# Output projection of a hybrid decoder layer: two tiles at once, seven block products in place of eight

## The chip, the cores and the metric

The kernel runs on one core of one Trainium2 chip. Each core has a matrix engine (PE, whose weight loads are shown as PEld), VectorE (DVE), ScalarE (ACT), GpSimd (POOL), and a queue engine (SP) that issues most transfers. Each engine works through its own instructions in order and waits on semaphores for the others. Results of PE land in PSUM (eight banks of 128x512 f32); everything else lies in SBUF or, outside the core, in DRAM. The metric is the device time of one execution in microseconds (us).

## The reference, cut to what matters

One decoder layer over 2048 tokens of width 1024, in f32. The change sits in the last two lines: `y` is 2048 x 1024, `w_out` is 1024 x 1024.

```python
h = rms_norm(x, pre_norm_g)
proj = h @ w_in                       # columns: a_u, a_v, sq, sk, sv, mq, z
y_a = chunked_spatial_gating(gelu(a_u), gelu(a_v), ...)   # 4 groups of 128 channels
y_b = sliding_window_attention(sq, sk, sv, sinks, rel_bias)
y_c = memory_cross_attention(mq, mk, mv)                  # 256 memory tokens
y = concatenate([y_a, y_b, y_c]) * silu(z)
x = x + rms_norm(y @ w_out, post_norm_g)
```

## The kernel before

The tokens are taken in four tiles (`t` = 0..3) of `TS` = 512. PE multiplies in a format that keeps only part of an f32 value, so each operand is split (`split`, L74 to L76) into a high part, rounded by ScalarE, and a low part, the difference, made by VectorE or GpSimd; a product is then three matmuls, high x high, high x low and low x high. One matmul here is 128x128 weights by 512 columns.

Weights come in units of 128 x 1024. `order` (L79 to L87) lists all units of all tiles in the order of use, and `weight_unit` (L129) keeps four units ahead: at first a unit is loaded as f32 from the input (`load_unit`, into the three places tagged `wraw`), split into one of four places tagged `whl`, and the split pair (1 MB) is stored to `split_d` in DRAM; later tiles load the pair from there. SP issues all of these, in program order.

A tile runs in stages:

- `v`: four units, 96 matmuls into four PSUM banks of the pool `ps_mm`, then GELU and normalisation on ACT, DVE and POOL.
- the groups `sv`, `k`, `q`, `mq`, `z`, `u` (`group`, L225), each 24 matmuls. Between the parts of a group, `slot()` runs pieces of the attention units: every unit of the window or memory attention has three stages (logits and softmax; transpose and split; product with the values), placed at fixed slot numbers by `A_SLOTS`. A tile has 60 slots, tile 0 has 68. What the slots issue for PE and SP stands in program order; the order on ACT, DVE and POOL is set by a planner that simulates the program.
- `finish` (L596) and `gate_a` (L647) make the eight 128-channel pieces of `y`, each split at once into the tile `y`.
- the output projection of the tile (L682 to L724): two halves `hf` of 512 output columns, 96 matmuls each into four banks `op`; while it runs, `load_h` (L217) loads, scales and splits the next tile's normalised `x` into `hT`, of which there is only one. Each half is squared (L715, for the norm) and multiplied by the norm's gain (L723) into `osb`; at the end `osb` is scaled, added to a fresh load of `x` and stored (L742 and, in the last tile, L749 to L755).

PE and SP follow the program's order exactly (`manual_schedule`).

Of the kernel before, what the change touches and what calls it, by code (L numbers as in the profile page):

```python
# [33 lines left out]
O_ORDER = (0, 2, 3, 1)  # L34
# [5 lines left out]
def kernel(  # L40
# [19 lines left out]
    cp = ctx.enter_context(tc.tile_pool(name="cp", bufs=1))  # L60
    wp = ctx.enter_context(tc.tile_pool(name="wp", bufs=4))
    sp = ctx.enter_context(tc.tile_pool(name="sp", bufs=2))

    tiny = ctx.enter_context(tc.tile_pool(name="tiny", bufs=2))
# [15 lines left out]
    for t in range(NT):  # L80
# [6 lines left out]
        order += [(U_O + 4 * hf + j, t) for hf in range(2) for j in O_ORDER]  # L87
# [5 lines left out]
    split_d = dram.tile([U_MK, P, 2, D], F32, name="split_d")  # L93
    stored_at = {u: 1 if u < U_SV else NT if u < U_MQ else 0 for u in range(U_MK)}
# [5 lines left out]
    def load_unit(i):  # L100
        u, t = order[i]
        if t > stored_at.get(u, 0):
            return
        raws[i] = raw_tile(f"wraw_{t}_{u}")
        for c in (slice(0, 512), slice(512, D)) if i == 0 else (slice(0, D),):
            nc.sync.dma_start(raws[i][:, c], wst[u][:, c])
            yield

    def split_unit(i):
        u, t = order[i]  # L110
        if i >= len(order) - 4:

            j = 2 * (i - len(order) + 4)
            w = hT[:, :, j : j + 2, :].rearrange("p s k n -> p s (k n)")
        else:
            w = wp.tile([P, 2, D], F32R, tag="whl", name=f"whl_{t}_{u}")
        ready[u, t] = w
        if i not in raws:
            nc.sync.dma_start(f32(w), split_d[u])
            return  # L120
# [8 lines left out]
    def weight_unit(u, t):  # L129

        i = order.index((u, t))
        while halved[0] < min(i + (4 if i < len(order) - 8 else 5), len(order)):
# [23 lines left out]

    ident = cp.tile([P, P], F32, name="ident")
# [20 lines left out]
    hT = cp.tile([P, 2, KC, TS], F32R, name="hT")  # L178
# [18 lines left out]
    def along(rstd, t):  # L197
# [5 lines left out]
        bcs = sp.tile([P, TS], F32, tag="bcs", name=f"bcs_{t}", bufs=1)  # L203
# [3 lines left out]
    def split_h(xk, k, bcs):  # L207

        g = g_pre[:, k : k + 1]
# [7 lines left out]
    def load_h(t, k, bcs):  # L217
        xk = sp.tile([P, TS], F32, tag="xk", name=f"xk_{t}_{k}", bufs=2)
        nc.sync.dma_start(xk, xT[t, k])
        split_h(xk, k, bcs)  # L220
# [4 lines left out]
    def group(w, t, tag, pool=None, slot=None):  # L225
# [4 lines left out]
        n = 0  # L230
        for k in range(KC):
# [13 lines left out]
    gpost_bc = cp.tile([P, D], F32, name="gpost_bc")  # L245
# [9 lines left out]
    def load_constants():  # L255
# [3 lines left out]
        nc.sync.dma_start(gpost_bc, gpost.broadcast_to([P, D]))  # L259
# [40 lines left out]
    def prep_memory():  # L300
# [14 lines left out]
        mT = sp.tile([P, 2, KC, MEM], F32R, tag="y", name="mT", bufs=1)  # L315
# [179 lines left out]

    for t in range(NT):

# [12 lines left out]
        for j in range(4):  # L510
            if t == 0:
                for kk in range(2):
                    split_h(xj[j][:, kk, :], 2 * j + kk, None)
# [7 lines left out]
            steps = [(i, *s) for i in range(4) for s in passes] if j == 3 else [(i, *s) for s in passes for i in range(4)]  # L521
            for i, hi, wi, kk in steps:
# [3 lines left out]
                                 stop=(j == 3 and (hi, wi, kk) == passes[-1]))  # L526
            if t == 0 and j == 0:
# [68 lines left out]
        def finish(name, k, z):  # L596

            for i in range(2):
                o = O[name][:, i, :]

                nc.vector.scalar_tensor_tensor(o, o, 0.5, ZB[z + i], ALU.mult, ALU.mult)
                split(y[:, 0, k + i, :], y[:, 1, k + i, :], o)
# [16 lines left out]
        at = [0]  # L619

        def slot(_=None):
            for stage, n in sorted(stages.pop(at[0], [])):
# [24 lines left out]
        def gate_a(g):  # L647
# [13 lines left out]
            split(y[:, 0, g, :], y[:, 1, g, :], af)  # L661
# [7 lines left out]
        y = sp.tile([P, 2, KC, TS], F32R, tag="y", name=f"y_{t}", bufs=1)  # L669
# [4 lines left out]
        if t + 1 < NT:  # L674
            for rstd_next in token_stats(t + 1):
                pass
        gate_a(2)
        gate_a(3)
        assert not stages


        rls = []  # L682
        ssp = tiny.tile([P, 2, 4], F32, tag="ssp", name=f"ssp_{t}")
        osb = [sp.tile([P, D], F32, tag=f"S{i}", name=f"osb_{t}_{i}", bufs=1) for i in range(4)]
        for hf in range(2):
            pool, tag = (ps_t, "t") if hf else (ps_mm, "mm")
# [147 lines left out]
```

## Time and profile before

| | |
|---|---|
| median of 3 runs | 799.35 us (798.95 to 799.65) |
| profiled execution, its own time | 799.43 us |
| its span, first to last instruction | 797.7 us |
| mean granted clock of PE | 0.993 |
| busy: PE / DVE / ACT / POOL | 783.7 / 496.2 / 368.4 / 160.9 us |
| moved by DMA | 169.05 MB, mean 212 GB/s |

The stages on PE, from the trace (us from the span's start): tile 0 up to its output projection 0 to 178.2, then the projection to 222.7; tile 1 to 368.9 and its projection to 413.3; tile 2 to 558.4 and to 602.9; tile 3 to 747.8 and to 791.5. The views are read like this: a row of the windows gives for a stretch its length, then each engine's busy time with its number of instructions, PE's granted clock, the DMA engines' busy share and rate. A row of the timeline gives start, duration, engine, line, operation, output<-inputs, shape and count, and in brackets the idle time before it with what ended it. A row of a tile gives the smallest, median and largest duration in ns. Busy time of PE counts overlapped, pipelined instructions, so a busy PE need not be at its peak rate.

### The profile page before, as it was taken

How to read it: one execution, taken by the hardware profiler on the slowest of the kernel's cores; microseconds unless marked ns; L12 is line 12 of the kernel's file. 1: busy time of each engine (PE TensorE's matmuls, PEld its weight loads, DVE VectorE, ACT ScalarE, POOL GpSimd, SP SyncE). 2: the span in 40 equal slices, each digit the busy share in tenths (PEclk: the TensorE clock that was granted, in tenths of full speed). 3: DMA queues.
4: the chain of work that ended last, by engine and by line, in shares of the span. 5: the costliest groups of instructions: out<-in, count | busy, mean ns of one | idle time of the engine just before them, and what ended most of it. 6: DMA issues, size and time to landing. Idle time of an engine off the chain costs nothing.

```text
span 797.7 us, 10520 instructions
## 1 busy us (share of the span) xinstructions
PE 783.7 (98%) x3884; PEld 660.0 (83%) x3884; DVE 496.2 (62%) x920; ACT 368.4 (46%) x816; POOL 160.9 (20%) x139
## 2 busy tenths in 40 slices
PE   9999999999999999999999999999999999999996
PEld 7878877888887888888888888888888888888885
DVE  6497899886546567775524466775624646777322
ACT  7785755753425544562314633473211653444221
POOL 4565442322223122000002203100000402200002
PEclk9999999999999999999999999999999999999999
DMA  8866465594898543555776453463759354334642
GB/s 324 312 219 221 141 239 185 202 370 144 321 358 322 208 159 128 207 194 184 246 295 226 161 184 129 159 229 141 257 217 375 121 191 159 123 142 159 234 188 105
DMA packets 36275, 169.05 MB, mean 212 GB/s; under 512 B 4187, under 2 KB 4736, under 8 KB 23936
## 3 DMA queue, kind: packets, MB, share of 16 engines
q1 hardware_dynamic: 33680, 160.97, 55.7%
q10 hardware_dynamic: 2544, 7.41, 2.3%
q8 instruction: 30, 0.49, 0.2%
q14 instruction: 21, 0.17, 0.1%
HBM read 132.71 MB, written 35.66 MB: 211 GB/s over the span
## 4 chain that ended last, share of the span: by engine, by line
PE 61%; issue 11%; DVE 7%; DMA 5%; POOL 2%; ACT 2%; SPq 0%; DVEq 0%; POOLq 0%; ACTq 0%
PE g_z L233 16%; PE op L694 12%; PE g_u L233 8%; PE v L523 5%; PE g_q L233 4%; PE g_mq L233 4%; DMA split_d<-whl 4%; PE g_k L233 2%; PE o_c L471 1%; PE l_b L400 1%; PE g_sv L233 1%; PE o_b L434 1%; PE l_c L450 1%; PE tp_c L465 1%; PE sg L652 1%
## 5 line engine op out<-in xcount | busy, mean ns | idle before, releaser
L233 PE MATMUL g_z<-hT,whl 128*128 128x512 f32 x768 | 196.0, 399 | 0.0
L233 PEld LDWEIGHTS g_z<-hT,whl 128*128 128x128 f32 x768 | 140.2, 191 | 25.7
L694 PE MATMUL op<-whl,y 128*128 128x512 f32 x672 | 153.9, 390 | 0.0
L694 PEld LDWEIGHTS op<-whl,y 128*128 128x128 f32 x672 | 125.7, 188 | 25.8
L76 POOL TENSOR_TENSOR whl<-wraw,whl 128x1024 fp32r<-128x1024 f32 x36 | 87.4, 2432 | 163.9 <-ACT whl L75 145.8
L233 PE MATMUL g_u<-hT,whl 128*128 128x512 f32 x384 | 97.2, 395 | 0.0
L523 PE MATMUL v<-whl,hT 128*128 128x512 f32 x384 | 88.6, 390 | 0.3 <-DVE hT L212 0.3
L523 PEld LDWEIGHTS v<-whl,hT 128*128 128x128 f32 x384 | 72.0, 188 | 16.4 <-DVE hT L212 0.7
L75 ACT CAST whl<-wraw 128x1024 fp32r<-128x1024 f32 (+1 forms) x51 | 52.7, 1033 | 66.3 <-DMA wraw<-in_wst 32.1
L233 PEld LDWEIGHTS g_u<-hT,whl 128*128 128x128 f32 x384 | 69.4, 188 | 12.9
L723 DVE TENSOR_TENSOR osb<-op,gpost_bc 128x512 f32<-128x512 f32 x32 | 21.4, 687 | 54.5 <-ACT jk L715 54.5
L715 ACT ACTIVATE jk<-op 128x512 f32<-128x512 f32 x32 | 19.0, 598 | 68.1 <-PE op L694 68.1
L424 POOL TENSOR_SCALAR_AFFINE_SELECT pp_b<-po_b 128x512 fp32r<-128x512 f32 x30 | 19.9, 664 | 141.5 <-ACT po_b L75 141.5
L233 PE MATMUL g_q<-hT,whl 128*128 128x512 f32 x192 | 45.9, 394 | 0.0
L233 PE MATMUL g_mq<-hT,whl 128*128 128x512 f32 x192 | 44.7, 389 | 0.0
L410 ACT ACTIVATE Lc_b<-Lc_b,nm_b 128x129 f32<-128x129 f32 x64 | 25.0, 393 | 42.4 <-DVE nm_b L408 42.4
L233 PEld LDWEIGHTS g_q<-hT,whl 128*128 128x128 f32 x192 | 35.7, 188 | 7.8 <-issue 0.5
L233 PEld LDWEIGHTS g_mq<-hT,whl 128*128 128x128 f32 x192 | 35.9, 188 | 7.3
L457 ACT ACTIVATE L_c<-l_c,nm_c 128x256 f32<-128x256 f32 x64 | 29.8, 471 | 26.1 <-DVE nm_c L455 26.0
L214 DVE SCALAR_TENSOR_TENSOR xk<-xk,colt,bcs 128x512 f32<-128x512 f32 x24 | 21.9, 949 | 17.2 <-DMA xk<-in_xT 16.8
L75 ACT CAST hT<-xk 128x512 fp32r<-128x512 f32 x24 | 14.9, 621 | 37.1 <-DVE xk L214 36.7
L153 POOL TENSOR_TENSOR rsr_o<-rsa_o,mhalf 128x4 f32<-128x4 f32 x3 | 3.0, 1013 | 139.0 <-DVE rsa_o L151 139.0
(181 smaller groups left out, 1229.4 us busy)
## 6 DMA issues: line engine op xcount, KB each, us to landing
whl<-split_d SPq DMA_DIRECT2D x70, 1024.0 KB, 4.8
split_d<-whl SPq DMA_DIRECT2D x26, 1024.0 KB, 8.1
wraw<-in_wst SPq DMA_DIRECT2D x49, 512.0 KB, 5.5
xs<-in_x SPq DMA_DIRECT2D x12, 512.0 KB, 4.1
xk<-in_xT SPq DMA_DIRECT2D x24, 256.0 KB, 3.1
xv<-in_x SPq DMA_DIRECT2D x8, 512.0 KB, 6.7
xr<-in_x SPq DMA_DIRECT2D x8, 512.0 KB, 8.1
hT<-split_d SPq DMA_DIRECT2D x4, 1024.0 KB, 8.9
```

The lines of the kernel that those rows point to most:

```text
L75: nc.scalar.copy(hi, src)
L76: (lo_engine or nc.vector).tensor_tensor(lo, src, f32(hi), ALU.subtract)
L214: nc.vector.scalar_tensor_tensor(xk, xk, g, bcs, ALU.mult, ALU.mult)
L233: nc.tensor.matmul(ps, w[:, wi, k * P : (k + 1) * P], hT[:, hi, k, :], start=(n == 0), stop=(n == 3 * KC - 1))
L400: nc.tensor.matmul(lg[:, e, :], S[kv][:, e, c * P : (c + 1) * P], KK[:, kv, s, c * P : c * P + 256], start=(s == 0), stop=(s == 1))
L410: nc.scalar.activation(Lc[:, h, : P + 1], Lc[:, h, : P + 1], AF.Exp, bias=nm[:, h : h + 1], accum_out=den[:, h : h + 1])
L424: nc.gpsimd.affine_select(prev[:, s], f32(own[:, s]), [[0, 4], [-1, P]], ALU.is_gt, 0.0, base=0, channel_multiplier=1)
L457: nc.scalar.activation(p[:, e, :], lg[:, e, :], AF.Exp, bias=nm[:, e : e + 1], accum_out=den[:, e : e + 1])
L523: nc.tensor.matmul(vps[i], hT[:, hi, 2 * j + kk, i * P : (i + 1) * P], w[:, wi, kk * 512 : (kk + 1) * 512], start=(j == 0 and (hi, wi, kk) ...
L694: nc.tensor.matmul(ops[i], y[:, hi, k, i * P : (i + 1) * P], w[:, wi, kk * 512 : (kk + 1) * 512], start=(j == O_ORDER[0] and kk == 0 and h ...
L715: nc.scalar.activation(junk, ops[i], AF.Square, accum_out=ssp[:, hf, i : i + 1])
L723: nc.vector.tensor_tensor(half, ops[i], gpost_bc[:, hf * 512 : (hf + 1) * 512], ALU.mult)
```

## The change

The output projection leaves the tile loop. In the loop each piece of `y` is stored to DRAM as f32 (`store_y`, six ticks later by `flush_y`; a tick is a slot) and not split. There are two places for `h` (`hTs`), so that `load_h` of the next tile runs in slots of the present one: in its last 28 slots the statistics, then `along`, then one `load_h` every second slot. Behind the last tile the pools of the loop are closed and a second phase does the projection for two tiles at a time (`p` = 0: tiles 0 and 1; `p` = 1: tiles 2 and 3). With A the 1024 x 1024 block of `y` of the two tiles and B the weights, both cut into 2 x 2 blocks of 512 x 512, it forms seven products for the eight of the plain form (each sum on VectorE, in two halves of 128 x 1024):

```
S1 = A21 + A22   S2 = S1 - A11   S3 = A11 - A21   S4 = A12 - S2
T1 = B12 - B11   T2 = B22 - T1   T3 = B22 - B12   T4 = B21 - T2
products, in order: S2.T2, S3.T3, A11.B11, A12.B21, S1.T1, A22.T4, S4.B22
```

Each product is 4 row blocks (`m`) of 12 matmuls; X and Y are banks that two products accumulate into. The weight operands (B11, B21, B22, T1 to T4, each in two halves) are made, split and stored to DRAM in slots of tiles 1 and 2 (`weight_operands`); S2 and S3 of the first pair in slots of tile 3 (`first_sums`). The eight units of the output weights no longer stand in `order`; T2 and T3 are its last four units. The core of the diff:

```diff
-        order += [(U_O + 4 * hf + j, t) for hf in range(2) for j in O_ORDER]
+    order += [("T2", 0), ("T2", 1), ("T3", 0), ("T3", 1)]
+    hTs = [hp.tile([P, 2, KC, TS], F32R, name=f"hT{i}") for i in range(2)]
+    def weight_operands(j, place):
...
+        def operand(op, r):
+            w = place[:, :, 2 * (n[0] % 4) : 2 * (n[0] % 4) + 2, :].rearrange("p s k n -> p s (k n)")
+            n[0] += 1
+            split(w[:, 0], w[:, 1], r, nc.gpsimd)
+            to_store.append((op, w))
...
+        def minus(out, a, b):
+            nc.vector.tensor_tensor(out, a, b, ALU.subtract)
...
+            by_bank = j == 3 or (j == 0 and t > 0)
...
-                nc.vector.scalar_tensor_tensor(o, o, 0.5, ZB[z + i], ALU.mult, ALU.mult)
-                split(y[:, 0, k + i, :], y[:, 1, k + i, :], o)
+                nc.vector.scalar_tensor_tensor(ZB[z + i], O[name][:, i, :], 0.5, ZB[z + i], ALU.mult, ALU.mult)
+                store_y(t, k + i, ZB[z + i])
...
+            for i in range(4):
+                jobs.setdefault(n_slots - 28 + 2 * i, []).append(stats_next)
+            jobs.setdefault(n_slots - 18, []).append(along_next)
+            for k in range(KC):
+                jobs.setdefault(n_slots - 17 + 2 * k, []).append(lambda k=k: load_h(t + 1, k, late["bcs_next"]))
+        if t:
+            side = first_sums(hTs[0]) if t == NT - 1 else weight_operands(t - 1, hTs[1 - t % 2]) if t < 3 else iter(())
+            for s in range(4, 32):
+                jobs.setdefault(s, []).append(lambda: next(side, None))
...
-            split(y[:, 0, g, :], y[:, 1, g, :], af)
+            store_y(t, g, af)
...
+    def operand(name, p):
+        A = {n: yraw[n, p] for n in ("11", "12", "21", "22") if (n, p) in yraw}
+        w = p2.tile([P, 2, 4, TS], F32R, tag="yop", name=f"yop_{name}_{p}", bufs=2)
+        for k in range(0, 4, 2):
...
+            split(w[:, 0, ks], w[:, 1, ks], src)
+    def norm_half(o, c, ss, col, p, tag):
+        nc.scalar.activation(junk, o[:, c], AF.Square, accum_out=ss[:, col : col + 1])
+        nc.vector.tensor_tensor(o[:, c], o[:, c], gpost_bc[:, c], ALU.mult)
+    def finish_rows(o, ss, xr, t, m, ends):
+        nc.vector.tensor_scalar(a, ss[:, 0:1], 1.0 / D, EPS, ALU.mult, ALU.add)
+        nc.vector.scalar_tensor_tensor(a, ss[:, 1:2], 1.0 / D, a, ALU.mult, ALU.add)
+        nc.gpsimd.tensor_tensor(r, a, mhalf2[:, 0:1], ALU.pow)
+        for c in (lo, hi) if ends else (slice(0, D),):
+            nc.vector.scalar_tensor_tensor(o[:, c], o[:, c], r, xr[:, c], ALU.mult, ALU.add)
+            (nc.sync if ends and c is lo else nc.scalar).dma_start(out[r0 : r0 + P, c], o[:, c])
...
+        for m in product(X, s2, pieces(T2), True):
+            nc.scalar.copy(osa[m][:, hi], X[m])
+        for m in product(X, s3, pieces(T3), False):
+            nc.scalar.copy(osb[m][:, lo], X[m])
...
+        for m in product(Y, a11, rows(B11), True):
+            nc.vector.tensor_tensor(osa[m][:, hi], Y[m], osa[m][:, hi], ALU.add)
+            nc.vector.tensor_tensor(osb[m][:, lo], osb[m][:, lo], Y[m], ALU.add)
...
+        for m in product(X4, a22, rows(T4), True):
+            nc.vector.tensor_tensor(osb[m][:, lo], X4[m], osb[m][:, lo], ALU.add)
+            norm_half(osb[m], lo, ssb[m], 0, p, f"b{m}_{p}_0")
+            finish_rows(osb[m], ssb[m], xrs[m], tb, m, False)
+            xrs.append(residual_load(*((tb, 3) if m == 0 else (ta, m - 1))))
+            if m == 1:
+                s4 = operand("S4", p)
+                if p == 0:
+                    load_y("22", 1)
+                    load_y("11", 1)
+        for m in product(Z, s4, rows(B22), False):
+            nc.vector.tensor_tensor(osa[m][:, hi], Z[m], osa[m][:, hi], ALU.add)
+            norm_half(osa[m], hi, ssa[m], 1, p, f"a{m}_{p}_1")
+            finish_rows(osa[m], ssa[m], xrs[4 + m], ta, m, p == 1 and m == 3)
+            if p == 0 and m == 1:
+                s2_next = operand("S2", 1)
+                load_y("12", 1)
+        if p == 0:
+            s3_next = operand("S3", 1)
+            B11 = load_operand("B11", 1, 0)
```

309 lines of the change are left out of this document (210 added, 99 removed).

## The prediction, written before the changed kernel ran

> **What bounds the kernel now.** I read the totals first, then the windows cut at the stages.
>
> ```profile
> span 797.7 us, 10520 instructions
> PE 783.7 (98%) x3884; PEld 660.0 (83%) x3884; DVE 496.2 (62%) x920; ACT 368.4 (46%) x816; POOL 160.9 (20%) x139
> 0.00:178.19 178.19, 170.96 (x873) 143.72 (x874) 146.12 (x242) 118.02 (x235) 77.28 (x53) 0.98 0.68 245
> 222.66:368.86 146.20, 145.59 (x742) 123.33 (x741) 93.44 (x191) 70.11 (x169) 26.29 (x27) 1.00 0.58 212
> 368.86:413.33 44.47, 44.47 (x201) 36.94 (x201) 19.82 (x30) 11.43 (x26) 0.00 (x0) 1.00 0.69 249
> 413.33:558.43 145.10, 145.10 (x741) 123.22 (x741) 89.11 (x189) 67.38 (x161) 21.55 (x25) 1.00 0.51 185
> ```
>
> PE bounds it: it sits idle 14.0 us in all, 7.2 of them in tile 0. VectorE is at 82% in tile 0, at 64% and 61% in the loops of tiles 1 and 2, and at 45% in a projection. So a projection (44.5 us) is also the time in which VectorE catches up, and this is what the change takes out of the loop. Next the rate of PE, from the chain that ended last:
>
> ```profile
> 375.21 38.12 PE op L694 x168
> ```
>
> 168 matmuls in 38.12 us are 0.227 us each; the 390 ns that the groups show is the length of one in the pipeline, not the spacing.
>
> **The change, part by part.** *Matmuls.* The projection has 768 (4 tiles of 192); afterwards it has 2 x 7 x 48 = 672. 96 fewer by 0.227 us are 21.8 us, all on the bound engine: **-21.8**. One product is 48 x 0.227 = 10.9 us.
>
> *Tile ends.* The next tile's h moves from the projection into the last 17 slots of tiles 0 to 2. Its price and its new surroundings:
>
> ```profile
> L214 DVE SCALAR_TENSOR_TENSOR xk<-xk,colt,bcs x24: 737/751/2448, 185.5 to 582.0; 128x512 f32<-128x512 f32 x24
> L76 DVE TENSOR_TENSOR hT<-xk,hT x24: 681/692/695, 188.6 to 583.9; 128x512 fp32r<-128x512 f32 x24
> L76 DVE TENSOR_TENSOR y<-a,y x16: 670/684/693, 121.0 to 750.7; 128x512 fp32r<-128x512 f32 x16
> 148.40:178.19 29.79, 29.79 (x166) 25.80 (x165) 25.28 (x41) 18.79 (x39) 8.20 (x4) 1.00 0.90 334
> 338.00:368.86 30.86, 30.86 (x170) 26.43 (x169) 18.80 (x35) 16.49 (x39) 1.01 (x1) 1.00 0.47 173
> 222.66:244.42 21.76, 21.76 (x97) 18.02 (x96) 11.26 (x15) 7.30 (x16) 5.77 (x3) 1.00 0.92 335
> ```
>
> Eight h steps are 8 x (0.75 + 0.69) = 11.5 us of VectorE, the copy behind `along` 0.7; two y splits go, -1.4. Tile 0's last stretch comes to 25.3 + 10.8 = 36.1 us of VectorE in 29.8 of PE: 6.3 too many. Tiles 1 and 2 come to 29.6 in 30.9: just full. Queued behind the h steps are the attention's splits; PE has three slots (some 5.5 us) between transposes and product there in tile 0, four later. The surplus itself can drain under the next tile's v stage: its row shows 11.3 of 21.8 us, and some of that is the old projection's tail. So 6.3 less 5.5: I take **+1** at tile 0's end, between 0 and 8 (no slack used, and a clock loss, below); nothing at the others, up to 3 each.
>
> *Weight operands.* Per tile seven splits on GpSimd and four subtractions on VectorE:
>
> ```profile
> L76 POOL TENSOR_TENSOR whl<-wraw,whl 128x1024 fp32r<-128x1024 f32 x36 | 87.4, 2432 | 163.9 <-ACT whl L75 145.8
> L76 DVE TENSOR_TENSOR whl<-wraw,whl x15: 692/1216/1226, 4.2 to 626.2; 128x1024 fp32r<-128x1024 f32 x13, 128x512 fp32r<-128x512 f32 x2
> 267.59:287.00 19.41, 19.41 (x96) 16.39 (x95) 12.33 (x24) 7.61 (x25) 0.00 (x0) 1.00 0.47 163
> 288.11 0.64 POOL L424 TENSOR_SCALAR_AFFINE_SELECT pp_b<-po_b 128x512 fp32r<-128x512 f32 x1 [25.95 <-ACT po_b L75]
> ```
>
> 17.0 us of GpSimd from slot 5 on, into a stretch where it has nothing, but with ACT and VectorE steps between they reach past 288, where the window attention's masks begin. One split ahead of a mask costs 2.4 us, which is about the slack. VectorE: 12.3 + 4.9 of 19.4. I take **+1** for each of tiles 1 and 2, 0 to 4 each.
>
> Here a rule speaks against the change. The trace:
>
> ```profile
> 95.94 5.16 DVE L407 TENSOR_TENSOR Lc_b<-L_b 128x256 f32<-128x256 f32 x2
> 95.87 4.94 POOL L76 TENSOR_TENSOR whl<-wraw,whl 128x1024 fp32r<-128x1024 f32 x2 [9.14 <-ACT whl L75]
> ```
>
> Two maxima that elsewhere take 0.4 us each are held until two GpSimd splits end. The Trainium skill, GPSIMD Engine Reference, § Specifications, says the same: GpSimd shares its SBUF interfaces with VectorE, and instructions with two SBUF inputs contend. The trace agrees here. What it would do is rival 4.
>
> *What leaves and what comes on the queues.* Gone are the splits of 32 y pieces, 8 weight splits in tile 0, and 36 MB (8 stores and 24 loads of 1 MB, 8 raw loads of 0.5 MB). New are 55 MB: y out (8) and back (8 + 3), weights raw (4), 14 operand stores, 18 operand loads. SP issues them; a y store is issued six slots after its emission (six matmuls or more each, so at least 8 us), and the weight loads queued behind it lead by three units (16 us). Cost 0; without that cover up to a landing each. Tile 1's loop goes from 212 to some 270 GB/s, below the 334 to 341 that rows here reach.
>
> *Start of phase 2.* The first two products (21.8 us) need only what is ready. A11 must be loaded and split by then, and SP sends ahead of it 2 MB of T3, 2 MB of B11, the last y pieces:
>
> ```profile
> 748.00:769.60 21.60, 21.60 (x96) 17.86 (x96) 5.50 (x9) 3.81 (x10) 0.00 (x0) 1.00 0.86 341
> hT<-split_d SPq DMA_DIRECT2D x4, 1024.0 KB, 8.9
> whl<-split_d SPq DMA_DIRECT2D x70, 1024.0 KB, 4.8
> ```
>
> 5.75 MB at 341 GB/s are 16.9 us, then cast and low part, some 4: 20.9 against 21.8. I take 0; the other end is rival 3.
>
> *The turn between the pairs.* Here I expect the one large wait. VectorE's prices:
>
> ```profile
> L723 DVE TENSOR_TENSOR osb<-op,gpost_bc 128x512 f32<-128x512 f32 x32 | 21.4, 687 | 54.5 <-ACT jk L715 54.5
> L715 ACT ACTIVATE jk<-op 128x512 f32<-128x512 f32 x32 | 19.0, 598 | 68.1 <-PE op L694 68.1
> L742 DVE SCALAR_TENSOR_TENSOR xr<-osb,rsr_o,xr 128x1024 f32<-128x1024 f32 x6 | 7.4, 1278 | 0.0
> L718 DVE SCALAR_TENSOR_TENSOR rsa_l<-ssp,sse 128x1 f32<-128x1 f32 x4 | 0.6, 160 | 16.1 <-ACT jk L715 16.1
> L721 POOL TENSOR_TENSOR rsr_l<-rsa_l,mhalf 128x1 f32<-128x1 f32 x4 | 2.2, 553 | 86.1 <-DVE rsa_l L718 86.1
> L75 ACT CAST whl<-wraw 128x1024 fp32r<-128x1024 f32 (+1 forms) x51 | 52.7, 1033 | 66.3 <-DMA wraw<-in_wst 32.1
> ```
>
> A row block of the last two products costs VectorE an add 0.69, the gain 0.69, two small 0.32 and the final 1.28: 2.98 us, where PE makes one every 2.73. As a chain, with the square (0.6 + 0.2), GpSimd's power (0.55) and hand-offs, it takes 4.6. The first pair starts at 0: A22.T4 runs from 54.5 to 65.4, S4.B22 to 76.3. The next pair's S2 (six sums and two low parts of 1.22: 9.8) can be formed only when y blocks 22 and 11 are in; their loads stand on SP behind a residual load that waits for row block 1 to finish (59.9 + 4.6 = 64.5), and land 8.9 later, 73.4. In VectorE's queue stand eight row blocks, S4 and S2. If S4 fills the idle time before 57.2, then six blocks (17.9) and S2 without its two late subtractions (7.4) end at 82.5: PE waits 6.2. With S4 (4.9) in line and everything of S2 it is 13.6; if S2 overtakes the row blocks, some 2. I take **+8**. A wait of this length also costs clock:
>
> ```profile
> 137.28 0.51 PE L471 MATMUL o_c<-pT_c,MV 128*128 128x256 f32 x2 [1.88 <-DVE pT_c L76]
> 137.97:144.24 6.27, 5.61 (x18) 4.01 (x18) 0.73 0.45 153
> 94.90 0.44 PE L364 MATMUL mvt<-ident,mvs 128*128 128x128 f32 x2 [0.99 <-ACT mvs L357]
> 95.09 3.00 PE L233 MATMUL g_u<-hT,whl 128*128 128x512 f32 x12
> ```
>
> Behind the wait of 1.88 us the granted clock is 0.73 over 6.27 us: 1.7 us lost. Behind 0.99 us twelve matmuls take their usual 3.0. So **+1.7** here and none for waits of 1 us. The Trainium skill, TensorE: Matmul & The Clock Gate, Part 1, has the clock halved only after an idle window of about 3.4 us; the row shows 1.88 us doing it. By the page the waits at tile ends would never cost clock, by the row three of them above 1.9 us would add 5.1 to the sum.
>
> *Tail.*
>
> ```profile
> 769.62 21.92 PE L694 MATMUL op<-hT,y 128*128 128x512 f32 x96
> ```
>
> PE ends at 791.5, 6.2 before the end. Afterwards the last block has an add (0.69) and a small step more, and VectorE has fallen behind by 8 x (2.98 - 2.73) = 2.0: **+2**, 1 to 6.
>
> The sum: 797.7 - 21.8 + 1 + 2 + 8 + 1.7 + 2 = 790.6 of span. The profiled execution took 799.43, 1.7 more than its span, and stands 0.1 over the median. **Forecast 792.3 us**, 0.9% faster; its own range is 786 to 798.
>
> **The rivals.**
>
> 1. *All of it hides.* The planner puts S2 ahead, the tile ends drain under v. For it: the loop's PE idles 0.6 us in tile 1 and nothing in tile 2, with VectorE at 64%. Against it: the row blocks alone exceed PE's pace. Only the tail stays: 797.7 - 21.8 + 2 + 1.7 = 779.6.
>
> 2. *VectorE's strict order makes the row blocks a chain (slower).* If the queue waits inside each row block for the square and the power, a block costs r between 2.98 and 4.6. With S4 in line the turn waits 57.2 + 6r + 14.7 - 76.3 = 6r - 4.4; the last pair's eight blocks and S4, from 57.2 of its own 76.3, lengthen the tail by 8r + 4.9 - 19.1 + 2 - 6.2 = 8r - 18.4. The 17.1 us left after the other terms are used up at 14r = 39.9, r = 2.85; with S4 in idle time, at about 3.55. For r = 3.7, in the middle: 797.7 - 21.8 + 3 + 1.7 + 29.0 + 1.7 = 811.3. For it: VectorE already waits 54.5 us in the old projection for the square. Against it: that is while PE is not done, and the order in the trace follows readiness.
>
> 3. *y comes back late (no change).* At the 249 GB/s of tile 1's projection the 5.75 MB take 23.1 us, with the split 27.1: PE waits 5.3 and loses 1.7 of clock. 792.3 + 7.0 = 799.3.
>
> 4. *GpSimd's splits hold VectorE in tiles 1 and 2 (slower).* If each of the seven holds an instruction for its whole length, VectorE needs 12.3 + 4.9 + 17.0 = 34.2 us in 19.4: 14.8 over, less some 5 of slack, 9.8 a tile instead of 1: 792.3 + 17.6 = 809.9. It decides from some 5 us a tile. Against it: most of VectorE's work there reads PSUM, and the splits wait for casts and loads in between. It is the rule of the Trainium skill, GPSIMD Engine Reference, cited above, fully paid.
>
> **How the numbers follow.** The forecast 0.38, rival 1 0.18, rival 2 0.20, rival 3 0.14, rival 4 0.10. A difference of 0.2% (1.6 us) is about what a measurement of this kernel can tell. Faster: 0.35 + 0.18 + 0.05 + 0.02 = 0.60; slower: 0.01 + 0.18 + 0.05 + 0.08 = 0.32; within: 0.08. The range 780 to 808 leaves out half of rival 1 and the upper half of rivals 2 and 4, some 2 in 10.
>
> **What would show it.** The group of projection matmuls has 672 instructions and covers 152 to 155 us of PE without waits. In the loop PE's waits stay under 5 us per tile, with VectorE above 90% in the last 30 us of tiles 0 to 2. In phase 2 the list of waits has one of 5 to 10 us, for the low part of S2 between the pairs, with the clock below 1 behind it. The tail is 7 to 12 us behind PE's last matmul. The prediction is wrong if that wait is missing or doubled, if PE waits for A11 at the phase's start, or if window attention in tiles 1 and 2 waits for masks by more than 4 us.

## The result and the profile after

The changed kernel takes 849.42 us (849.29 to 850.11) against 799.50 for the kernel before on the same chip: 1.0627 times as long, 95% interval 1.0609 to 1.0645. The forecast of 792.3 us, and its range up to 808, were wrong. One of the four executions of experiment 13 below took 1552.16 us, in a slower state, and is left out of that experiment's figures. The totals of the page after:

```profile
span 847.5 us, 10587 instructions
PE 781.2 (92%) x3788; PEld 653.8 (77%) x3788; DVE 578.6 (68%) x1004; ACT 395.2 (47%) x839; POOL 198.4 (23%) x155
```

PE was at 98%. It has 96 matmuls fewer, and now sits idle for 66 us. The windows cut at the stages (tiles 0 to 3, each from its first v matmul to the next tile's, then the second phase up to PE's last matmul; columns as before) say where:

```profile
0.00:185.73 185.73, 173.59 (x880) 145.45 (x881) 154.64 (x249) 117.66 (x234) 77.63 (x53) 0.98 0.67 236
185.73:349.41 163.68, 150.18 (x750) 126.83 (x749) 109.60 (x205) 76.86 (x171) 43.13 (x32) 0.96 0.66 243
349.41:513.18 163.77, 151.03 (x750) 127.56 (x749) 104.33 (x198) 75.25 (x169) 43.10 (x32) 0.95 0.62 225
513.18:661.97 148.79, 146.93 (x742) 124.40 (x741) 93.89 (x188) 64.59 (x152) 20.51 (x22) 0.99 0.49 177
661.97:837.31 175.34, 159.51 (x674) 129.60 (x672) 110.59 (x157) 59.61 (x111) 12.01 (x14) 0.93 0.59 223
```

| us | before | after | difference |
|---|---|---|---|
| tile 0 without projection | 178.2 | 185.7 | +7.5 |
| tile 1 | 146.2 | 163.7 | +17.5 |
| tile 2 | 145.1 | 163.8 | +18.7 |
| tile 3 | 144.9 | 148.8 | +3.9 |
| four projections / second phase | 177.1 | 175.3 | -1.8 |
| behind PE's last matmul | 6.2 | 10.2 | +4.0 |

The last but one row hides two things: 672 matmuls at 0.227 us are 152.5, so the products themselves save 24.6, and 22.9 of waits and lower clock come back. PE's list of waits (line waited for, total us, times, longest) names them:

```profile
PE g_u L238 <- DMA whl<-split_d: 18.4, 2, 9.5
PE tp_b L420 <- DVE Lc_b L416: 9.7, 3, 4.0
PE X L873 <- ACT yop_S L80: 8.6, 1, 8.6
PE o_c L474 <- DVE pT_c L81: 6.4, 3, 3.0
PE X L873 <- DVE yop_S L81: 4.6, 2, 4.1
PE X L873 <- ACT oa L920: 2.6, 1, 2.6
```

*The largest, g_u, once in each of tiles 1 and 2.* Four engines' timelines of the kernel after, in tile 1 (start, duration, engine, line, operation, idle time before it and what ended it): SP's, GpSimd's, ScalarE's, PE's.

```profile
254.28 0.52 SPq L517 DMA_DIRECT2D wo_T<-hT  x1
271.06 0.52 SPq L517 DMA_DIRECT2D wo_B<-hT  x1
278.55 0.51 SPq L517 DMA_DIRECT2D wo_T<-hT  x1
279.15 17.40 SPq L122 DMA_DIRECT2D whl<-split_d  x5
...
268.48 2.55 POOL L81 TENSOR_TENSOR hT<-wo,hT 128x1024 fp32r<-128x1024 f32 x1
275.59 2.93 POOL L81 TENSOR_TENSOR hT<-wo,hT 128x1024 fp32r<-128x1024 f32 x1 [4.56 <-ACT hT L80]
...
265.04 1.05 ACT L80 CAST hT<-wo 128x1024 fp32r<-128x1024 f32 x1
...
286.42 6.53 PE L238 MATMUL g_u<-hT,whl 128*128 128x512 f32 x18 [9.54 <-DMA whl<-split_d]
```

Read it from the end. PE waits 9.54 us for a weight load. That load left SP at 279.15, right behind the store of operand T4 (278.55), which could go only when GpSimd had made T4's low part (275.59 + 2.93). Before it SP stood 16.3 us at the store of B21 (254.28 to 271.06). GpSimd made B21's low part at 268.48, right behind masks, but these account only for the 2.4 us before it: the cast on ScalarE that the low part needs had run at 265.04, and SP itself had issued the load of block 21 as late as 252.09. T4 is formed in the place of that block, and its subtraction on VectorE came at 273.22. So SP, in program order, issued no weight load from 254.3 to 279.2. Eighteen matmuls behind the wait take 6.53 us where 18 elsewhere in the trace take 4.11: 2.4 us of clock besides. In tile 2 the same wait is 8.90 us.

*The second, tp_b.* VectorE's timeline at the first window unit's softmax, GpSimd's beside it, and PE's row behind it:

```profile
238.31 2.96 DVE L410 TENSOR_TENSOR Lc_b<-L_b 128x256 f32<-128x256 f32 x2
242.64 3.23 DVE L521 TENSOR_TENSOR wo<-wo,wo 128x1024 f32<-128x1024 f32 x2
245.97 3.29 DVE L521 TENSOR_TENSOR wo<-wo,wo 128x1024 f32<-128x1024 f32 x1
249.18 2.83 DVE L416 TENSOR_TENSOR Lc_b<-Lc_b,den_b 128x512 f32<-128x512 f32 x1
...
238.47 5.06 POOL L81 TENSOR_TENSOR hT<-wo,hT 128x1024 fp32r<-128x1024 f32 x2 [18.28 <-ACT hT L80]
245.77 8.48 POOL L81 TENSOR_TENSOR hT<-wo,hT 128x1024 fp32r<-128x1024 f32 x3 [2.25 <-ACT hT L80]
...
252.16 0.63 PE L420 MATMUL tp_b<-ident,Lc_b 128*128 128x128 f32 x4 [3.97 <-DVE Lc_b L416]
```

While GpSimd's splits run (238.5 to 243.5 and 245.8 to 254.3), two maxima take 2.96 us where they take 0.4 each elsewhere, the third subtraction takes 3.29 where one of its shape takes 1.22 (L863, below), and the unit's own multiplication 2.83 for 0.69. They are all operations on two SBUF operands. This is the hold of rival 4, in a place where it hurts, with the subtractions queued in front of the softmax; this trace does not separate the two. Together they cost 3.97 and some 1.6 of clock: with 9.54 + 2.4, tile 1's 17.5.

*In the second phase.* ScalarE's row at its start, PE's rows there and between the pairs, SP's at the loads of y for S2, and VectorE's at the sums of S2:

```profile
675.00 2.06 ACT L920 COPY oa<-X 128x512 f32<-128x512 f32 x4 [12.31 <-DMA yd<-Z_z]
...
675.64 12.80 PE L873 MATMUL X<-whl_T,hT 128*128 128x512 f32 x48 [2.60 <-ACT oa L920]
751.47 1.22 PE L873 MATMUL X<-whl_T,yop_S 128*128 128x512 f32 x2 [8.63 <-ACT yop_S L80]
756.75 2.93 PE L873 MATMUL X<-whl_T,yop_S 128*128 128x512 f32 x6 [4.06 <-DVE yop_S L81]
760.22 22.70 PE L873 MATMUL X<-whl_T,yop_S 128*128 128x512 f32 x88 [0.54 <-DVE yop_S L81]
...
732.77 1.34 SPq L830 DMA_DIRECT2D y<-yd  x2
...
743.99 2.36 DVE L862 TENSOR_TENSOR s<-y,y 128x1024 f32<-128x1024 f32 x2 [1.46 <-DMA y<-yd]
749.06 1.22 DVE L863 TENSOR_TENSOR s<-s,y 128x1024 f32<-128x1024 f32 x1 [1.44 <-DMA y<-yd]
```

The first copy out of X writes memory that the loop's pool held; ScalarE waits 12.31 us until the last store of y has read it, and PE, out of banks, 2.60. At the turn blocks 22 and 11 of the next pair are there at 744.0 and 749.1, not at 73.4 from the phase's start (735.4). SP issued both loads from 732.77 on, behind the residual load that waits for row block 1, and they were there 11.2 and 16.3 us later. Behind them S3's two subtractions and parts of two row blocks stand on VectorE ahead of S2's first low part (755.48). PE waits 13.2 us and, at a lower clock, takes some 5 more.

### The profile page after: what moved, and what is told of

Read it like the earlier page. It is cut to its first block, busy times and chain, and to the rows that moved or that the text cites. A ratio compares the mean times of both kernels' runs of the same rounds, so it can differ in the third digit from the quotient of the medians.

```text
span 847.5 us, 10587 instructions
## 1 busy us (share of the span) xinstructions
PE 781.2 (92%) x3788; PEld 653.8 (77%) x3788; DVE 578.6 (68%) x1004; ACT 395.2 (47%) x839; POOL 198.4 (23%) x155
## 4 chain that ended last, share of the span: by engine, by line
PE 60%; DVE 17%; DMA 7%; issue 2%; ACT 2%; POOL 1%; SPq 1%; DVEq 0%; ACTq 0%; POOLq 0%
PE g_z L238 12%; PE g_u L238 8%; PE v L611 8%; PE X L873 6%; PE Y L873 5%; PE g_q L238 4%; PE Z L873 3%; DVE Lc_b L410 2%; DMA yd<-Z_z 2%; PE g_mq L238 2%; PE g_k L238 2%; PE g_sv L238 2%; DMA y<-yd 2%; DVE wo L521 2%; DMA whl<-split_d 2%
## 5 line engine op out<-in xcount | busy, mean ns | idle before, releaser
L81 POOL TENSOR_TENSOR whl<-wraw,whl 128x1024 fp32r<-128x1024 f32 x32 | 77.9, 2438 | 207.2 <-ACT whl L80 192.3
L238 PE MATMUL g_u<-hT,whl 128*128 128x512 f32 x384 | 104.9, 419 | 18.4 <-DMA whl<-split_d 18.4
L897 POOL TENSOR_TENSOR r<-a,mhalf 128x1 f32<-128x1 f32 x16 | 14.0, 879 | 215.4 <-DVE a L894 182.7
L80 ACT CAST whl<-wraw 128x1024 fp32r<-128x1024 f32 (+1 forms) x43 | 44.2, 1028 | 42.8 <-PE v L611 32.0
L81 POOL TENSOR_TENSOR hT<-wo,hT 128x1024 fp32r<-128x1024 f32 x14 | 37.6, 2699 | 50.7 <-ACT hT L80 50.7
L873 PE MATMUL Z<-hT,yop_S 128*128 128x512 f32 x192 | 44.2, 389 | 0.0
L873 PE MATMUL Y<-hT,yop 128*128 128x512 f32 x192 | 43.8, 389 | 0.0
L873 PEld LDWEIGHTS Y<-hT,yop 128*128 128x128 f32 x192 | 36.0, 188 | 7.5
L873 PEld LDWEIGHTS Z<-hT,yop_S 128*128 128x128 f32 x192 | 36.0, 188 | 7.5
L81 DVE TENSOR_TENSOR yop<-y,yop 128x1024 fp32r<-128x1024 f32 x12 | 14.2, 1222 | 40.0 <-ACT yop L80 40.0
## 6 DMA issues: line engine op xcount, KB each, us to landing
hT<-wo_B SPq DMA_DIRECT2D x10, 1024.0 KB, 10.9
```

Of the source, the lines that this page charges most:

```text
L80: nc.scalar.copy(hi, src)
L81: (lo_engine or nc.vector).tensor_tensor(lo, src, f32(hi), ALU.subtract)
L238: nc.tensor.matmul(ps, w[:, wi, k * P : (k + 1) * P], hT[:, hi, k, :], start=(n == 0), stop=(n == 3 * KC - 1))
L873: nc.tensor.matmul(ops[m], a(s, k)[:, m * P : (m + 1) * P], b(w, k), start=first and n == 0, stop=n == 11, skip_group_check=not first)
L897: nc.gpsimd.tensor_tensor(r, a, mhalf2[:, 0:1], ALU.pow)
```

## The experiments

Each was timed beside the kernel before on the same chip, and the ratio is to that kernel, with its 95% interval. Experiments 1 to 4, 5 to 8, 9 to 11, 12 and 13, 14 and 15 ran on five chips, on which the kernel before took 798.65 to 799.64 us. Waits and stage times come from one profiled execution of each kernel.

**1. The stores out of the loads' way.** In `weight_operands`:

```diff
         operand("T4", b21)
-        yield
-        yield
-        yield
+        for _ in range(20):
+            yield
         store()
```

> The last two operand stores of tiles 1 and 2 (B21 and T4) are issued at slot 31 in place of 14; nothing else moves. Theory A (SP's queue): PE's waits of 9.5 and 8.9 us for a g_u weight load come from SP, which stands at these stores until GpSimd's low parts are done (271 and 278 us) while the weight loads are queued behind; both waits go, and the clock lost behind them (2.2 us each), so some 23 us: 849.4 to about 826. The waits of 4.0 and 3.8 us for the softmax (tp_b) stay. Rival B (GpSimd holding VectorE sets the pace of these tiles): the weight wait is replaced by waits for attention steps and the gain is under 8 us. Rival C (the DMA rings are full there): the wait stays, no change.

Measured 829.73 us, 1.0381 [1.0356, 1.0405], 19.7 less than the kernel after. Both waits for weights are gone. The softmax's stays; PE's row:

```profile
256.40 0.63 PE L420 MATMUL tp_b<-ident,Lc_b 128*128 128x128 f32 x4 [4.13 <-DVE Lc_b L416]
```

So the queue is shown as the largest single cause, theory A. Tile 1 still takes 156.0, which is 9.8 more than before (in an execution of 832.93 us, the longest of the four).

**2. The hold away.** Low parts of the weight operands on VectorE:

```diff
-            split(w[:, 0], w[:, 1], r, nc.gpsimd)
+            split(w[:, 0], w[:, 1], r)
```

> The low parts of the seven weight operands are formed by VectorE (1.22 us each) in place of GpSimd (2.4 to 2.9 us); stores stand where they stood. Theory A: the splits no longer queue behind the window masks on GpSimd, the stores' waits shorten, and of the 23 us at the weight loads most goes. Theory B (GpSimd holds VectorE instructions with two SBUF inputs): the waits of 4.0 and 3.8 us for the softmax and 4 us of clock behind them go as well. Both: 849.4 to 815 to 825. If instead VectorE's load decides (8.5 us more per tile), the softmax waits grow to 6 us or more and the gain stays under 15.

Measured 827.48, 1.0340 [1.0317, 1.0363]. The waits for weights go here too: SP issues the stores of B21 and T4 at 264.4 and 268.9 in place of 271.1 and 278.6. The softmax waits longer, against theory B; PE's row:

```profile
253.43 1.09 PE L420 MATMUL tp_b<-ident,Lc_b 128*128 128x128 f32 x4 [5.34 <-DVE Lc_b L416]
```

VectorE's own extra work in front of the softmax costs as much as GpSimd's hold did. So the 21.9 us gained come from the waits for weights.

**3. y earlier.** The loads of blocks 22 and 11 of the second pair moved ahead of the product A22.T4:

```diff
         load_y("21", 1)
+        load_y("22", 1)
+        load_y("11", 1)
...
-            load_y("22", 1)
-            load_y("11", 1)
```

> The loads of y blocks 22 and 11 of the second pair are issued before the product A22.T4 in place of behind its second row block; SP then does not stand at residual loads ahead of them. Theory D (late data): S2 of the second pair is late because block 11 lands at 749.1, 6.4 us after PE is ready for it (742.7); with the data 15 us earlier the wait of 13.2 us falls to 2 to 5, and with the clock behind it the gain is 9 to 14 us: 835 to 840. Rival E (VectorE's in-order queue: row blocks, S3's subtractions and the final steps stand ahead of S2's low parts): the wait falls by no more than the 6 us of the late data, 842 to 845.

Measured 845.64, 1.0576 [1.0541, 1.0611], 3.8 less than the kernel after, near rival E. The wait does not go, it changes its name; PE's row, ScalarE's and VectorE's:

```profile
767.62 5.49 PE L873 MATMUL X<-whl_T,yop_S 128*128 128x512 f32 x12 [9.39 <-ACT oa L920]
...
766.98 0.59 ACT L920 COPY oa<-X 128x512 f32<-128x512 f32 x1 [6.72 <-DMA out<-oa]
...
758.33 1.27 DVE L900 SCALAR_TENSOR_TENSOR oa<-oa,r,xr 128x1024 f32<-128x1024 f32 x1
```

Now the copy out of X waits for the first row block of `oa` of the first pair to be stored. VectorE finishes that row block at 759.6 only; its residual had been requested at 747.17, and VectorE had worked without a pause since 735. So here VectorE's own queue is late, and not a transfer.

**4. `oa` first in the second phase's memory.**

```diff
+    oa_first = [p2.tile([P, D], F32, tag=f"oa{m}", name=f"oa{m}_0") for m in range(4)]
     load_y("11", 0)
```

> In the second phase's pool the four tiles oa are placed first, so that they lie on the memory of the loop's constants and not on the last y pieces. Theory: ScalarE's first copies out of X wait 12.3 us for the store of the last y piece, whose memory oa takes over, and PE waits 2.6 us for the banks, with 1.8 of clock behind it: a gain of 4 us, 845. Rival: something else of the new memory is as late (A11's load then lands on it): no change, or PE waits at A11.B11.

(The tile `gpost_bc` moves behind them.) Measured 850.26, 1.0625 [1.0604, 1.0647]: no change, where 845 was expected. ScalarE's row shows the old wait with `oa` at another address:

```profile
677.60 2.05 ACT L921 COPY oa<-X 128x512 f32<-128x512 f32 x4 [12.30 <-DMA yd<-Z_z]
```

This fits an old pool that comes free as a whole, with its last reader; two places were tried, so it is not shown for every one.

**5. Operands spread out, on VectorE.** One operand about every four slots from slot 4 to 31, with the edit of 2.

> The weight operands of tiles 1 and 2 are made one every four slots from slot 4 to 31 (in place of all between slots 5 and 13), low parts on VectorE, each store at least three slots behind its split. Theory (place of the work: a burst in front of the first window's softmax, and stores on SP ahead of the weight loads): both kinds of wait go, the softmax ones to under 1.5 us a tile; of the 35 us lost in tiles 1 and 2 some 32 come back: about 817. Rival (VectorE's sum is too much for the loop without the projection's time): waits come back at other attention steps and the time stays at or above the 827 of the low parts on VectorE alone.

Measured 836.62, 1.0459 [1.0431, 1.0488], worse than experiment 2 and far from the 817 of the theory: spread out evenly, the work meets the softmax (5.23 us of wait in each of tiles 1 and 2) and the masks (3.7 us in all) as well.

**6. The turn.** 3 with two more edits: the last y pieces are stored ahead of the phase's weight loads, and `oa` and `ob` swap places in the second pair, so that the copy needs the place stored first.

```diff
+    flush_y(True)
     T2 = [weight_unit("T2", j) for j in range(2)]
...
-        osa = [p2.tile([P, D], F32, tag=f"oa{m}", name=f"oa{m}_{p}") for m in range(4)]
+        osa = [p2.tile([P, D], F32, tag=f"o{'ab'[p]}{m}", name=f"oa{m}_{p}") for m in range(4)]
```

> Second phase only: the last y pieces are stored before B11 is loaded; blocks 22 and 11 of the second pair are loaded before A22.T4; in the second pair oa and ob exchange places, so that the copies out of X go to the places that were finished first. Theory (each of the three waits is a transfer queued behind something that it does not need): the wait of 2.6 us for the first copies goes, the turn's wait falls from 13.2 to under 3, the clock behind them (6.4) goes too: 849.4 less some 20, 829. Rival (VectorE is behind by its row blocks at the turn, whatever the order): a wait of 5 to 9 us stays at the turn, 838.

Measured 836.43, 1.0462 [1.0442, 1.0482], 13.0 less than the kernel after, between the theory's 829 and the rival's 838. PE's rows at the turn:

```profile
743.61 20.24 PE L873 MATMUL X<-whl_T,yop_S 128*128 128x512 f32 x88 [0.68 <-DVE yop_S L81]
768.08 7.27 PE L873 MATMUL Y<-hT,yop 128*128 128x512 f32 x20 [4.24 <-DMA hT<-wo_B]
```

The waits at S2.T2 are 0.38 and 0.68 where they were 13.2, as the theory had it. PE's wait for the copies at the phase's start is gone too, and 88 matmuls take 20.24 where they took 22.70 behind the wait. The next thing that is late is B11, whose reload stands on SP behind the residual loads: 4.24 us, and 20 matmuls in 7.27 for 4.5. That is about what is missing to the 829.

**7 and 8. Both phases.** 7 is 5 and 6 together; 8 the same with the low parts on GpSimd.

> The two edits together (operands spread with low parts on VectorE; second phase's transfers reordered). If the losses are separate, the gains add: 817 + 829 - 849 = 797, level with the kernel before. If they share a cause (VectorE's load), less than the sum: above 805.

> As the two edits together, but with the low parts of the weight operands on GpSimd again. Theory (GpSimd's splits hold VectorE's instructions with two SBUF inputs): VectorE has 8.5 us less of work a tile, but is held by seven splits of 2.4 us; 5 to 14 us slower than with the low parts on VectorE. Rival (only the burst mattered): the same time or up to 3 us faster.

Measured 820.88, 1.0266 [1.0245, 1.0286], and 817.06, 1.0221 [1.0203, 1.0239]. The measured gains of 5 and 6, 12.8 and 13.0 us, add up to 823.6, so the two losses do not share a cause; 797 was not reached because neither gain was the expected one. Experiment 8 goes against its theory of 5 to 14 us more: at this spacing GpSimd is the better place by 3.8 us, with no wait for the softmax in tiles 1 and 2. Left is the product's wait for masks that stand behind a split on GpSimd, and at the end a residual load in its ring of three places; PE's row, and one of the chain that ended last:

```profile
262.13 0.58 PE L437 MATMUL o_b<-po_b,SV 128*128 128x256 f32 x1 [3.06 <-POOL po_b L429]
...
803.51 7.01 DMA xr<-in_x
```

**9. What is left in phase 2.** Edits to 8:

```diff
-            B11 = load_operand("B11", 1, 0)
+            B11 = load_operand("B11", 1, 0, nc.scalar)
...
-        xrs = [residual_load(tb, m) for m in range(3)]
+        xrs = residual_pairs(tb) + residual_pairs(ta) if p else [residual_load(tb, m) for m in range(3)]
```

(The last argument is the queue, ScalarE's in place of SP's; `residual_pairs` loads two residual tiles into each place tagged `whl`.)

> e8_both_pool with two edits in phase 2: the reload of B11 for the second pair is issued on ScalarE's queue instead of behind the residual loads on SP, and the second pair's eight residual tiles are loaded ahead into the four weight places that T2 and T3 leave free, instead of through the ring of three. Theory (what is left in phase 2 is SP's order): the wait of Y for B11 (4.1 us and some 2.5 of clock) goes, and the last row block no longer waits for its residual, so the tail goes from 10.9 to some 8: 817.1 - 9.5 = 807 to 809. Rival (VectorE's row blocks, 2.98 us each where TensorE makes one every 2.73, set phase 2's end, and the loads only fill the time): TensorE ends earlier but the tail grows by as much, no more than 3 us gained: 814 to 817.

Measured 808.79, 1.0124 [1.0090, 1.0158]: 8.3 us less than experiment 8, the theory. The wait for B11 is gone from PE's list; PE takes 154.0 us for the second phase, where 152.5 would be its matmuls alone, and the tail goes from 10.9 to 9.1.

**10. Tile 0's h steps four slots apart.** Edit to 8, which also moves tile 0's statistics and `along` 15 slots ahead:

```diff
-                jobs.setdefault(n_slots - 28 + 2 * i, []).append(stats_next)
-            jobs.setdefault(n_slots - 18, []).append(along_next)
+                jobs.setdefault((n_slots - 28 if t else 25) + 2 * i, []).append(stats_next)
+            jobs.setdefault(n_slots - 18 if t else 35, []).append(along_next)
...
-                jobs.setdefault(n_slots - 17 + 2 * k, []).append(lambda k=k: load_h(t + 1, k, late["bcs_next"]))
+                jobs.setdefault(n_slots - 17 + 2 * k if t else 37 + 4 * k, []).append(lambda k=k: load_h(t + 1, k, late["bcs_next"]))
```

> e8_both_pool with one edit: in tile 0 the eight h steps for the next tile stand four slots apart from slot 37 on, instead of two apart in the last 17 slots. Theory (tile 0's loss is 11.5 us of VectorE work bunched in its last 30 us): the waits of o_c for its low part, 6.7 us in tile 0, fall to 1 to 2, tile 0 ends 4 to 6 us earlier: 811 to 813. Rival (VectorE is full in all of tile 0, 153 of 182 us, so the work delays other units wherever it stands): waits of the same size at other places, 815 to 819.

Measured 813.19, 1.0175 [1.0145, 1.0205]: 3.9 less than experiment 8. PE's list of waits has, of the 6.7 us for `o_c` in 8,

```profile
PE o_c L474 <- DVE pT_c L81: 5.2, 4, 3.8
```

so the theory held in part: the later waits of the tile nearly went, the first and longest stayed (3.81 for 3.02). An earlier wait, for `mvt` at 97 us, grew from 0.99 to 2.02. Tile 0 ends 3.3 us earlier than in 8; among the kernels that leave tile 0 alone (the kernel after and 1 to 9) its end lies anywhere from 185.6 to 188.7 us, so this difference is about as large as the scatter of single executions.

**11. All of it, and the splits behind the masks.** 9 and 10 together; each GpSimd split two slots behind the call of a window unit's masks (three of them ahead of the first), `along` and the h steps one slot later, the first sums from slot 34.

> Both edits of e9_phase2, the one of e10_tile0, and three in tiles 1 to 3: each GpSimd split of a weight operand is called two slots behind the call of a window unit's masks instead of ahead of them (B11, T1 and B22 before the first masks; T3, T2, B21, T4 one per window unit); the copy behind along and the h steps stand one slot later; the first sums of tile 3 start at slot 34, behind the window units, instead of slot 4. Theory (all that is left of the loss are splits in front of masks, 8.8 us of clock and waits in tile 1 and 9.2 in tile 2, the bunched h steps in tile 0, 2 in tile 3, and SP's order in phase 2): 817.1 - 9.5 - 5 - 16 - 1.5 = 785, faster than the kernel before. Rival (GpSimd's splits hold VectorE wherever they stand, and its work lacks room in these stretches): half of the 16 in tiles 1 and 2 stays, 792 to 797.

Measured 802.40, 1.0040 [1.0024, 1.0056], against 785 expected and 792 to 797 of the rival: the mask waits went, and the softmax's came back. All three subtractions ran on VectorE between that softmax's own steps (239.5 to 246.8). PE's row:

```profile
249.67 1.09 PE L420 MATMUL tp_b<-ident,Lc_b 128*128 128x128 f32 x4 [3.87 <-DVE Lc_b L416]
```

**12 and 13. Clear of the softmax and of the masks.** The side work starts ahead of the sv group and goes on between the parts of k and q (`early(i)` is `next(side, None)`): B11 and T1 there, B22 and T3 in slots 0 to 2, then T2, B21 and T4 in slots 17, 22 and 27. In 13 VectorE makes the low parts.

```diff
-        svs = group(weight_unit(U_SV, t), t, f"sv{t}", ps_t, rstd_along)
+        early(0)
+        svs = group(w_sv, t, f"sv{t}", ps_t, rstd_along)
...
-        ps = group(weight_unit(U_K, t), t, f"k{t}", ps_t)
+        ps = group(weight_unit(U_K, t), t, f"k{t}", ps_t, early)
```

> e11_all with the weight operands called from the sv group on: B11, T1, B22 and T3 with all three of their subtractions before the first window unit's logits (slot 7), then nothing until its masks are called, then T2, B21 and T4 one per window unit; along and the h steps one slot later again. Theory (the 3.9 us wait for the first softmax, and the clock behind it, come of GpSimd splits and subtractions that stand inside that unit's steps): the wait goes in tiles 1 and 2, 6 to 7 us each, and tiles 1 and 2 take 147 us: 802.4 - 13 = 788 to 790, faster than the kernel before. Rival (VectorE has no room for it in this stretch wherever it stands): the wait moves to the k and q groups or a later unit, 797 to 802.

> e12_early with the seven low parts made by VectorE instead of GpSimd. Theory (what counts is that the work stands clear of the first softmax and the masks, not which engine does it): within 2 us of e12_early, since VectorE is at some half of its time in the sv, k and q groups. Rival (the hold by GpSimd is a cost at any place): 3 to 6 us faster than e12_early. Second rival (VectorE is what is short, 8.6 us more per tile): 3 to 8 us slower.

Measured 788.76, 0.9868 [0.9849, 0.9886], and 787.46, 0.9853 [0.9830, 0.9876]: 1.3 to 1.5% faster than the kernel before, and the theories' numbers. The windows of 12 for tiles 1 and 2 and for the second phase:

```profile
185.76:332.63 146.87, 146.49 (x750) 124.23 (x749) 101.94 (x198) 73.62 (x168) 41.66 (x32) 1.00 0.71 257
332.63:478.80 146.17, 146.17 (x749) 124.16 (x749) 102.61 (x199) 74.71 (x169) 42.36 (x32) 1.00 0.71 252
623.92:777.90 153.98, 152.94 (x672) 125.64 (x671) 110.28 (x157) 59.10 (x111) 16.54 (x14) 1.00 0.69 261
```

Tiles 1 and 2 are back within 1.1 us of the kernel before (146.2 and 145.1), with all seven operands made in them. That 13 is as fast says that neither the hold in 12 nor VectorE's extra work in 13 costs PE much at these places. The groups of the subtractions (count, busy, mean ns) in the kernel after, in 12 and in 13:

```profile
L521 DVE TENSOR_TENSOR wo<-wo,wo 128x1024 f32<-128x1024 f32 x8 | 15.9, 1982 | 0.1
...
L521 DVE TENSOR_TENSOR wo<-wo,wo 128x1024 f32<-128x1024 f32 x8 | 11.4, 1423 | 0.8 <-DMA wo<-in_wst 0.8
...
L521 DVE TENSOR_TENSOR wo<-wo,wo 128x1024 f32<-128x1024 f32 x8 | 10.6, 1325 | 1.0 <-DMA wo<-in_wst 0.9
```

The calls stand clear of softmax and masks, but in 12 not all the work does. GpSimd's row in tile 1, and VectorE's at the first window unit's multiplication:

```profile
242.11 2.41 POOL L81 TENSOR_TENSOR hT<-wo,hT 128x1024 fp32r<-128x1024 f32 x1 [11.86 <-ACT hT L80]
...
243.84 1.23 DVE L416 TENSOR_TENSOR Lc_b<-Lc_b,den_b 128x512 f32<-128x512 f32 x1
```

The split still runs beside that softmax and holds the multiplication (1.23 for 0.69), and PE does not wait for it. What is gone from among the softmax's steps are the three subtractions and some of the splits. No run moves the subtractions alone, so how much of the gain is theirs stays open.

**14 and 15. Tile 0, with less work on VectorE.** 12 with GpSimd making, in 14, the low parts of tile 0's eight h steps, in 15 all low parts of raw weights behind the first unit, some of which VectorE had made. The edit of 14:

```diff
-            split(hT[:, 0, k, :], hT[:, 1, k, :], xk)
+            split(hT[:, 0, k, :], hT[:, 1, k, :], xk, nc.gpsimd if t == 1 else nc.vector)
```

> e12_early with the low parts of tile 0's eight h steps (for tile 1) made by GpSimd. Theory (VectorE's own time is short at tile 0's end, 19 of 20 us busy from 120 to 160): 5.5 us less on it, the waits of o_c (5.2 us) fall by half or more, tile 0 ends 3 to 5 us earlier: 784 to 786. Rival (every GpSimd operation holds VectorE's operations on two SBUF operands, so the time comes back as holds): 788 to 791.

> e12_early with all low parts of raw weights behind the first unit made by GpSimd; before, VectorE made every third. Theory (VectorE short): some 1.22 us less for each on VectorE in tile 0, 785 to 787. Rival (holds, and weights that come later because GpSimd takes 2.4 us for each): 789 to 793, with waits for whl in tile 0.

Measured 788.44, 0.9875 [0.9859, 0.9892], and 788.52, 0.9868 [0.9853, 0.9883], as 12. Tile 0 ends at 184.3 and 183.0 where it ended at 185.8, and the second phase starts at the same 623.2 and 623.9. PE's waits for `o_c` in 14:

```profile
PE o_c L474 <- DVE pT_c L81: 4.1, 3, 3.3
PE o_c L474 <- ACT pT_c L80: 1.8, 1, 1.8
```

They sum to 5.9 us, in 12 to 6.2, in 15 to 4.9. Neither theory is shown: less work on VectorE hardly shortens these waits, the earlier ends of tile 0 differ by no more than the scatter named under 10, and whether the time returns as holds can't be told from these runs. Why the low part for the first `o_c` product is late stays open.

## Why the prediction was wrong, step by step

The term of each step, and what was measured in the kernel after:

- *Matmuls, -21.8.* Right: -24.6 without waits. In experiment 12 the second phase takes 154.0 us of PE where four projections took 177.1.
- *What leaves and what comes on the queues, "Cost 0; without that cover up to a landing each".* **This step failed**, and it is the largest miss: 9.54 + 2.4 us in tile 1, 8.90 + 2.4 in tile 2. The 16 us of lead were taken as cover for transfers. But an SP store also waits for what makes its data, and here that was a chain over a late load, ScalarE's cast and GpSimd's low part. SP stood 16.3 us at one store and 7.0 at the next, together more than the lead. The prediction asked when the stores of y could be issued (six slots after their emission), but of the 14 operand stores only what they move, and not for how long SP would stand at them. Experiment 1 moved the last two stores of each tile and got 19.7 us back.
- *Weight operands, +1 for each of tiles 1 and 2.* Mis-sized: in the kernel after 5.6 us of tile 1 are not the queue's, and in experiment 1, without the queue, tile 1 is 9.8 longer than before. Rival 4 had the mechanism but put it on the total of VectorE's time; the time was lost where side work, held or not, stood in front of a softmax or a mask. The experiments show that the place decides: the same work makes tile 1 longer by 8.1 us in 2, by 14.4 in 5, and by 0.7 and 0.1 in 12 and 13. Which engine makes the low parts matters less: 3.8 us between 7 and 8, and 1.3 between 12 and 13. The rule of the Trainium skill, GPSIMD Engine Reference, § Specifications, that instructions with two SBUF inputs contend with GpSimd, agrees with the held rows above, 2.83 us for an operation of 0.69. Experiment 12 shows that such a hold need not cost PE anything.
- *Tile ends, +1.* Mis-sized: +7.5 in tile 0, near the upper end of 8. In 10 the whole kernel gained 3.9, but tile 0 of 12, with the same spacing, still ends 7.6 us later than before. The cause stays open.
- *Tile 3* had no term: +3.9, among it a wait for the softmax behind the first sums (1.86); from slot 34 on they cost +0.2 (12).
- *Start of phase 2, 0 for A11.* A11 came in time. Not seen was that the phase's memory is the loop's memory: 2.60 us of PE's wait and 1.9 of clock, gone in 6 with the early stores.
- *The turn, +8 and +1.7 of clock.* Right in place and in kind, half in size: 13.2 and some 5 (two of its own sums are off by 0.1: 6.1 and 13.5 follow from its terms). The order on SP was as predicted: the loads were issued 70.8 us after the phase's start where it had 64.5, and 4.5 of the difference is the late start. Too short was the landing, 11.2 and 16.3 us for 8.9; why it took so long is not shown. And S2's low parts stood behind S3's subtractions and row blocks on VectorE. With the loads moved and the places swapped (6) PE waits about 1 us for S2.
- *Clock.* The waits of 2.6 us and over that are shown here cost 1.6 to 2.8 us behind them; 1.7 had been taken from one row. Shorter ones are uneven: behind 2.02 us in 10 the granted clock is 0.70 over 9.8 us, behind 1.86 in tile 3 twelve matmuls take 4.58 us for 3.0, but behind 2.28 us in 12 and 1.91 in 8 it is 1.00. The Trainium skill, TensorE: Matmul & The Clock Gate, Part 1, has the drop come only after some 3.4 us idle; here it came behind 2.60, and 48 matmuls took 12.80 us for 10.88.
- *Tail, +2.* Measured +4.0, and +3.0 with the residual loads out of the way (12): 1 us more than VectorE's lag was reckoned at.

By these terms 6.5 (tile 0), 34.2 (tiles 1 and 2), 3.9 (tile 3), 4.5 (start of phase 2), 8.6 (turn) and 2.0 (tail) were missed, less 2.8 for the matmuls: 56.9 of the 57.1 us between 792.3 and 849.4. That 12, the same computation with its side work placed well, stands at 788.8 and so near the forecast is in part luck: its tile 0 costs 7.6 where 1 was taken, and its turn about 1 where 9.7 was taken.

## What to carry to other kernels

A store on a queue that works in order costs what its producer is late, and everything behind it pays; ask of each transfer that is added not how long it takes but when it can be issued, and what stands behind it then. Side work for an engine with spare time is not priced by its total: look for the few chains in which the main engine has little slack (here the first softmax and the masks), and put the work where none of them runs. When a wait is taken away, expect another in its place, as in experiments 3, 6 and 11, and follow them to the end before the version is judged.

## What was unexpected of the hardware

GpSimd's small power (one value per partition) takes 0.54 us, and 1.45 us in three of the last row blocks. Two of GpSimd's rows there, in the kernel after:

```profile
831.82 0.54 POOL L897 TENSOR_TENSOR r<-a,mhalf 128x1 f32<-128x1 f32 x1 [2.98 <-DVE a L895]
835.34 1.45 POOL L897 TENSOR_TENSOR r<-a,mhalf 128x1 f32<-128x1 f32 x1 [0.48 <-DVE a L895]
```

Each of the longer ones began 0.2 us behind the final step of a row block on VectorE (1.28 us, L900, both operands in SBUF) and ended 0.4 us behind it. So the hold seems to go both ways; where the two meet, a row block's chain is longer by 0.9 us.
